# Order of the slabs in the channel stage, and the per-layer gate of the token pair as seven products

## The chip, the cores and the metric

The kernel runs on one core of a Trainium2 chip. The metric is the device time of one execution in microseconds (us); the time given is the median of several runs. The engines are TensorE (PE, matmuls; its weight loads are shown apart as PEld), VectorE (DVE), ScalarE (ACT), GpSimd (POOL) and SyncE (SP), whose queue issues most transfers. They run side by side and wait for each other by semaphores.

## The reference

One layer of a decoder: a mixing part (attention and pooling heads), then a gated feed-forward part, then a per-layer input that is gated by the residual. The change touches the last two.

```python
def _rms(x, g):
    xf = x.astype(jnp.float32)
    y = xf * lax.rsqrt(jnp.mean(xf * xf, axis=-1, keepdims=True) + EPS)
    return (y * g.astype(jnp.float32)).astype(x.dtype)
...
    x = x + _rms(mix, n_mix_post)
    f = _rms(x, n_ffn_pre)
    f = (jax.nn.silu(f @ w_gate) * (f @ w_up)) @ w_down
    x = x + _rms(f, n_ffn_post)
    x = x + jax.nn.sigmoid(x @ w_ple_gate) * (p @ w_ple)
```

The width is 1024, the feed-forward width 2816 (22 chunks of 128), p has 256 columns. 1024 prompt tokens and 32 sample tokens make 1056.

## The kernel before

The tokens stand in the free dimension, as three groups of 352; groups 0 and 1 are called the pair. Activations are kept as halves of 512 features (a tile of 128x1408 is four blocks of 352). Every product is float32 made of three matmuls in a reduced float32 type: an operand is split into a rounded part (ScalarE cast, line 171) and a remainder (VectorE subtraction, line 172), and `gemm` issues hi x hi, hi x lo and lo x hi. So a product over 1024 features of one 128-wide chunk and one group is 24 matmuls of 352 columns. In the names, `wr` is a raw weight, `wh`/`wl` its two parts, `fh`/`fl` those of an activation, `hid` the hidden activations, `pl` those of p, `b` a PSUM bank (there are eight), `o` the sum of the down products, `sg` the gate.

For the pair, gate and up of one chunk are computed together by a scheme with seven half-width products where eight would be needed (84 matmuls in place of 96): the weights' sums S1 to S4 are formed by `w_sums` (line 1001: four 128x512 sums on GpSimd, written over the raw weights, then cast and remainder `sh`/`sl`), the activations' sums T1 to T4 once by `t_sum` (line 960, VectorE). Group 2 uses the plain 24-matmul products. Twenty-two chunks are walked as eleven slabs of two. `WALK` lists which groups take which slab when: with AHEAD = 5, slabs 0 to 4 for group 2 alone, slabs 5 to 10 for all three groups, then slabs 0 to 4 for the pair alone. After a slab, `downs` adds its down products (48 matmuls for each group) to `o`; after the last one of a group it forms squares for the norm, and `ple_steps` makes the residual x2 (a multiply at line 1126, four steps at line 1130 per half), splits it into an operand, and loads and splits p.

Per chunk m and group, `ple_out` then computes the gate (24 matmuls), the embedding product of p (6 matmuls), the sigmoid, a multiply and an add to x2 (lines 1175 to 1181), and writes the output.

Weights come through a list of items in the order of use. `need` keeps four items ahead: it loads a raw weight into one of three `wr` buffers, splits it into two of the eight `wp` tiles, and, for an item of kind "sums", calls `w_sums`. TensorE's instructions stand in the order of the code. The side work (norms, residuals) is written as chains of steps that are handed out between matmuls (`turn`, `chain`), by the VectorE time that `share` grants; VectorE, ScalarE and SyncE execute their queues in the order that the scheduler gave.

Of the kernel before, what the change touches and what calls it, by code (L numbers as in the profile page):

```python
# [10 lines left out]
F32 = mybir.dt.float32  # L11
# [28 lines left out]
AHEAD = 5  # L40
# [21 lines left out]
def trunk_kernel(  # L62
# [158 lines left out]
    WALK += [(s, (0, 1, 2)) for s in range(AHEAD, NSLAB)]  # L221
    WALK += [(s, (0, 1)) for s in range(AHEAD)]
# [6 lines left out]
    def direct_item(src, shape):  # L229
        return item("direct", add_plan(src, shape))  # L230

    WGU, WD = [], []
    for s, gs in WALK:
        pairs_of = []
        for i in range(SLAB):
# [4 lines left out]
            if i == 0 and WD:  # L240
                last_s = WALK[len(WD) - 1][0]
                WD[-1] = [direct_item(w_dn[last_s, j], [P, SLAB, 512]) for j in range(2)]
            if 0 in gs:
                ju = direct_item(w_gu[c, 1], [P, KC, P])
# [4 lines left out]
    WPE = [[], []]  # L249

    def plan_ple(n, m):
        wp = direct_item(w_ple[m // 4], [P, 2, 512]) if m % 4 == 0 else WPE[n][-1][0]
        WPE[n].append((wp, direct_item(w_pg[m], [P, KC, P])))

    FIRST = 1
    for m in range(FIRST):
        plan_ple(0, m)
    WD[-1] = [direct_item(w_dn[WALK[-1][0], j], [P, SLAB, 512]) for j in range(2)]
    for m in range(FIRST, KC):
        plan_ple(0, m)  # L260

    WPE[1] = [None] * 6 + WPE[0][6:]
    wp = WPE[0][-1][0]
    for m in reversed(range(6)):
        if m == 3:
            wp = direct_item(w_ple[0], [P, 2, 512])
        WPE[1][m] = wp, direct_item(w_pg[m], [P, KC, P])

    made = {}

    def need(k, ahead=LOOK):

        for i in range(len(made), min(k + ahead + 1, len(ITEMS))):
            kind, js = ITEMS[i]
            if kind == "direct":
                w_split(js[0])
                made[i] = pairs[js[0]]
            else:
                made[i] = w_sums(*(raws[ITEMS[j][1][0]] for j in js))
            for kind, js in ITEMS[i + 1 : i + 3]:  # L280
                if kind == "direct":
# [626 lines left out]
    def ffn_steps(g):  # L908
# [11 lines left out]
        for h in range(2):  # L920
# [7 lines left out]
            if (g, h) == (1, 0):  # L928
                t_sum("T1")
# [8 lines left out]
        if g == 1:  # L938
            for name in ("T3", "T2", "T4"):
                t_sum(name)  # L940
                yield 20, 0

# [9 lines left out]
    def t_sum(name):  # L952
        (b11, b21), (b12, b22) = ys[0], ys[1]
        out, a, b = {
            "T1": (b11, b12, b11),
            "T3": (b12, b22, b12),
            "T2": (b22, b22, b11),
            "T4": (b21, b21, b22),
        }[name]
        ve.tensor_tensor(out, a, b, op=ALU.subtract)  # L960
        f7[name] = f_operand(out, 0)
# [55 lines left out]
    def gate_up(items, slot, gs, pending):  # L1017
# [270 lines left out]
```

## Time and profile before

| | |
|---|---|
| median of 3 runs | 1115.65 us (1115.2 to 1115.71) |
| profiled execution, span | 1115.2 us |
| granted TensorE clock, by stretches from 350 us on | 1.00 |
| VectorE busy, us per 100, from 400, 600, 800, 900 | 49.0, 54.8, 83.3, 76.8 |
| weight loads of the channel part and the gate (512 KB each) | 64 + 32 + 14 |
| last stretch of the profile with GpSimd work | up to 1000 us |

The trace gives for each engine when an instruction ran and what it waited for. The chain of waits is followed back from the last instruction: at each step to what released it. Groups of instructions have one row for each line, operation and shape, with their number, busy time and mean duration in ns. The matmuls of a TensorE row overlap, so the pace is read from the count in a stretch and not from the mean. GpSimd's first weight sum starts at 386.14 us, with the first slab of all groups; the pair's slabs alone end, and the gate begins, shortly before 1000 us.

### The profile page before, as it was taken

What the parts mean: (1) busy time and instruction counts of PE and PEld (TensorE: products, weight loads), DVE (VectorE), ACT (ScalarE), POOL (GpSimd) and SP (SyncE); (2) the same over time, 40 slices, a digit from 0 to 9 for tenths busy, and PEclk for the clock granted to TensorE, in tenths of its full rate; (3) what the DMA queues carried; (4) which work ended last, traced back from release to release, by engine and by line L of the source; (5) the groups of instructions that cost most, each with busy time, mean ns of one, the idle gap of its engine ahead of it and who ended that gap; (6) DMA issues with size and microseconds to landing.
All of it is one profiled execution on the core that took longest, in us unless ns stands there. A gap on an engine that the chain in (4) does not pass through costs nothing.

```text
span 1115.2 us, 17663 instructions
## 1 busy us (share of the span) xinstructions
PE 1105.2 (99%) x7147; PEld 1089.1 (98%) x7147; DVE 748.6 (67%) x1241; ACT 440.4 (39%) x779; POOL 179.9 (16%) x156
## 2 busy tenths in 40 slices
PE   8999999999999999999999999999999999999998
PEld 8999988899999999999999999999999999999998
DVE  5767478886979955255464555547887877789532
ACT  6423276665645523331221313123424334366220
POOL 0045032200000131011111101111232123100000
PEclk9999999999999999999999999999999999999999
DMA  8121311542543212121110212122112222346211
GB/s 289 58 70 41 121 42 38 195 161 81 209 160 129 98 38 76 39 76 38 39 59 18 78 37 77 38 95 84 57 58 79 73 76 77 118 155 210 85 58 39
DMA packets 35217, 99.54 MB, mean 89 GB/s; under 512 B 4132, under 2 KB 14660, under 8 KB 35136
## 3 DMA queue, kind: packets, MB, share of 16 engines
q1 hardware_dynamic: 33808, 96.65, 25.7%
q10 hardware_dynamic: 1328, 1.77, 0.5%
q8 instruction: 56, 0.92, 0.4%
q14 instruction: 25, 0.20, 0.1%
HBM read 88.30 MB, written 10.11 MB: 88 GB/s over the span
## 4 chain that ended last, share of the span: by engine, by line
PE 94%; DVE 3%; DMA 1%; POOL 1%; issue 0%; ACT 0%; SPq 0%; DVEq 0%; POOLq 0%
PE b L126 93%; PE b L120 1%; DMA a<-in_dmask_dram 1%; DMA xr<-in_x_dram 1%; DVE wl L172 1%; POOL wr L1001 0%; DVE o L1126 0%; DVE x L1130 0%; DVE mx L639 0%; DVE a L747 0%; DVE p L1035 0%; DVE hid L172 0%; POOL a L653 0%; DVE sl L172 0%; ACT sh L171 0%
## 5 line engine op out<-in xcount | busy, mean ns | idle before, releaser
L126 PE MATMUL b<-fh,wh 128*128 128x352 f32 x808 | 260.8, 323 | 0.0
L126 PE MATMUL b<-fl,wh 128*128 128x352 f32 x808 | 258.8, 320 | 0.0
L126 PE MATMUL b<-fh,wl 128*128 128x352 f32 x808 | 258.8, 320 | 0.0
L126 PE MATMUL b<-hid,wh 128*128 128x352 f32 x1056 | 252.6, 322 | 1.8 <-DVE o L1126 1.2
L171 ACT CAST wh<-wr 128x1024 fp32r<-128x1024 f32 (+1 forms) x139 | 142.7, 1030 | 245.3 <-PE b L126 197.1
L172 DVE TENSOR_TENSOR wl<-wr,wh 128x1024 fp32r<-128x1024 f32 (+1 forms) x139 | 170.4, 1229 | 56.2 <-ACT wh L171 52.2
L126 PEld LDWEIGHTS b<-hid,wh 128*128 128x128 f32 x1056 | 182.3, 188 | 2.6 <-issue 1.5
L126 PE MATMUL b<-hid,wl 128*128 128x352 f32 x528 | 169.0, 320 | 0.0
L1001 POOL TENSOR_TENSOR wr<-wr 128x512 f32<-128x512 f32 x44 | 63.3, 1439 | 622.7 <-DVE wl L172 620.9
L126 PEld LDWEIGHTS b<-fl,wh 128*128 128x128 f32 x808 | 151.9, 188 | 0.0
L126 PEld LDWEIGHTS b<-fh,wh 128*128 128x128 f32 x808 | 151.5, 188 | 0.0
L126 PEld LDWEIGHTS b<-fh,wl 128*128 128x128 f32 x808 | 151.4, 187 | 0.0
L1098 DVE TENSOR_TENSOR o<-o,b 128x352 f32<-128x352 f32 x240 | 115.0, 517 | 28.9 <-PE b L126 28.7
L126 PE MATMUL b<-fh,sh 128*128 128x352 f32 x352 | 113.6, 323 | 0.0
L126 PE MATMUL b<-fl,sh 128*128 128x352 f32 x352 | 112.7, 320 | 0.0
L126 PE MATMUL b<-fh,sl 128*128 128x352 f32 x352 | 112.7, 320 | 0.0
L126 PE MATMUL b<-h,wh 128*128 128x352 f32 x480 | 106.0, 326 | 1.7 <-ACT h L372 1.4
L172 DVE TENSOR_TENSOR sl<-wr,sh 128x1024 fp32r<-128x1024 f32 x44 | 53.8, 1223 | 75.9 <-ACT sh L171 75.9
L126 PEld LDWEIGHTS b<-hid,wl 128*128 128x128 f32 x528 | 98.9, 187 | 0.0
L171 ACT CAST sh<-wr 128x1024 fp32r<-128x1024 f32 x44 | 45.7, 1047 | 131.2 <-POOL wr L1001 92.0
L126 PEld LDWEIGHTS b<-h,wh 128*128 128x128 f32 x480 | 82.3, 190 | 3.0 <-ACT h L372 1.8
L126 PE MATMUL b<-h,wl 128*128 128x352 f32 x240 | 66.4, 326 | 0.0
(153 smaller groups left out, 1590.7 us busy)
## 6 DMA issues: line engine op xcount, KB each, us to landing
wr<-in_w_gu_dram SPq DMA_DIRECT2D x64, 512.0 KB, 3.3
wr<-in_w_dn_dram SPq DMA_DIRECT2D x32, 512.0 KB, 3.5
wr<-in_w_pg_dram SPq DMA_DIRECT2D x14, 512.0 KB, 3.5
x<-in_x_dram SPq DMA_DIRECT2D x6, 704.0 KB, 7.0
x1d<-x SPq DMA_DIRECT2D x6, 704.0 KB, 3.5
x<-x1d SPq DMA_DIRECT2D x6, 704.0 KB, 6.6
out_y_dram<-yo SPq DMA_DIRECT2D x24, 176.0 KB, 1.9
wr<-in_w_out_b_dram SPq DMA_DIRECT2D x8, 512.0 KB, 3.3
```

Of the source, the lines that this page charges most:

```text
L120: ins = te.transpose(out, src, ident)
L126: ins = te.matmul(*args, **kw)
L171: fix(se.copy(hi, src))
L172: fix(ve.tensor_tensor(lo, src, hi.bitcast(F32), op=ALU.subtract))
L1001: ge.tensor_tensor(out, a, b, op=op)
L1098: ve.tensor_tensor(o, o, v, op=ALU.add)
```

## The change

AHEAD is 6, and no slab is shared any more: six slabs for group 2 alone, all eleven for the pair alone, then the last five for group 2. `gate_up` is parted into `seven` (the seven products, with a callback for each finished quarter), `gate_up_pair` and `gate_up_one`. For the pair, the second raw weight is split only by half (an item of kind "half", 128x512), since only its last quarter enters a product by itself. The sums T1 to T4 go to GpSimd. The per-layer gate of the pair now uses `seven` too, on two chunks of the gate's weight at a time: `pair_steps` makes x2 of the pair during group 2's last slabs, stores it to memory (`x2d`), forms a second set of T sums (`x27`) and splits their operands; `ple_pair` reads x2 back and runs the embedding product of each quarter (`embed`, 6 matmuls) as it is finished. `ple_pair(0)` comes before group 2's last downs, the other three after them, then `ple_one` does group 2's eight chunks. `share` is 0.35 and 0.5 where it was 0.1 and 0.7.

```diff
-AHEAD = 5
+AHEAD = 6
...
-    WALK += [(s, (0, 1, 2)) for s in range(AHEAD, NSLAB)]
-    WALK += [(s, (0, 1)) for s in range(AHEAD)]
+    WALK += [(s, (0, 1)) for s in range(NSLAB)]
+    WALK += [(s, (2,)) for s in range(AHEAD, NSLAB)]
+    LAST = {g: max(n for n, (_, gs) in enumerate(WALK) if g in gs) for g in range(G)}
...
+    def half_item(src):
+        return item("half", add_plan(src, [P, KC, P]))
...
-                ju = direct_item(w_gu[c, 1], [P, KC, P])
+                ju = half_item(w_gu[c, 1])
...
+    WP2, WPE = [], [None] * KC
+    for i in range(KC // 2):
+        wp = direct_item(w_ple[i // 2], [P, 2, 512]) if i % 2 == 0 else WP2[-1][0]
+        jg = direct_item(w_pg[2 * i], [P, KC, P])
+        ju = half_item(w_pg[2 * i + 1])
+        WP2.append((wp, jg, ju, item("sums", jg, ju)))
+        if i == 0:
+            WD[-1] = dn_items(len(WALK) - 1)
+    LATE = (*range(4, KC), *range(4))
+    for m in LATE:
+        if m == 0:
             wp = direct_item(w_ple[0], [P, 2, 512])
-        WPE[1][m] = wp, direct_item(w_pg[m], [P, KC, P])
+        WPE[m] = wp, direct_item(w_pg[m], [P, KC, P])
...
+            elif kind == "half":
+                w_load(js[0])
+                hl = w_tile([P, 4, P], "wh"), w_tile([P, 4, P], "wl")
+                split(*hl, raws[js[0]][:, 4:8, :])
+                made[i] = hl
...
-                t_sum("T1")
+                t_sum("T1", f7, ys[0], ys[1], flat(ys))
...
-        ve.tensor_tensor(out, a, b, op=ALU.subtract)
-        f7[name] = f_operand(out, 0)
+        ge.tensor_tensor(out, a, b, op=ALU.subtract)
+        b7[name] = f_operand(out, 0)
...
+    def product(w, x):
+        ps = bank()
+        gemm(ps[:, :N], ops4(w, x))
+        turn(12)
+        return ps[:, :N]
+
+    def direct(w, xs2):
+        ps = bank()
+        gemm(ps[:, :N], ops8(w, xs2))
+        turn(24)
+        return ps[:, :N]
+
+    def add(out, a, ps):
+        ve.tensor_tensor(out, a, ps, op=ALU.add)
+
+    def seven(items, x7, done):
 
         ig, iu, is_ = items
-        n = N
-
-        def product(w, x):
-            ps = bank()
-            gemm(ps[:, :n], ops4(w, x))
-            turn(12)
-            return ps[:, :n]
-
-        def direct(w):
-            ps = bank()
-            gemm(ps[:, :n], ops8(w, fs[2]))
-            turn(24)
-            return ps[:, :n]
-
-        def add(out, a, ps):
-            ve.tensor_tensor(out, a, ps, op=ALU.add)
-
         wg = need(ig)
-        if 0 in gs:
-            p1 = tmp(n, "p1")
-            se.copy(p1, product(quarter(wg, 0), f7["B11"]))
-        if 2 in gs:
-            sl = tmp(n, "sl")
-            se.activation(sl, direct(wg), AF.Silu)
-        if 0 in gs:
-            c11 = tmp(n, "c11")
-            add(c11, p1, product(quarter(wg, 1), f7["B21"]))
-            se.activation(c11, c11, AF.Silu)
-        if pending and 0 in gs:
-            pending()
-        wu = need(iu)
-        if 2 in gs:
-            ve.tensor_tensor(sl, sl, direct(wu), op=ALU.mult)
-        for g in gs:
-            if slot == 0:
-                new_hid[g] = half(g, F32R, "hid")
-        if 2 in gs:
-            hid_put(2, slot, sl)
-        if pending and 0 not in gs:
-            pending()
-        if 0 not in gs:
-            return
-        if 2 not in gs:
-            p4 = product(quarter(wu, 1), f7["T4"])
+        p1 = tmp(N, "p1")
+        se.copy(p1, product(quarter(wg, 0), x7["B11"]))
+        c11 = tmp(N, "c11")
+        add(c11, p1, product(quarter(wg, 1), x7["B21"]))
+        done("C11", c11)
+        p4 = product(need(iu), x7["T4"])
         s = need(is_)
-        add(p1, p1, product(s["S2"], f7["T2"]))
-        u3 = tmp(n, "u3")
-        add(u3, p1, product(s["S3"], f7["T3"]))
-        c21 = tmp(n, "c21")
-        if 2 in gs:
-            p4 = product(quarter(wu, 1), f7["T4"])
+        add(p1, p1, product(s["S2"], x7["T2"]))
+        u3 = tmp(N, "u3")
+        add(u3, p1, product(s["S3"], x7["T3"]))
+        c21 = tmp(N, "c21")
         add(c21, u3, p4)
-        ve.tensor_tensor(c21, c21, c11, op=ALU.mult)
-        hid_put(0, slot, c21)
-        p5 = product(s["S1"], f7["T1"])
+        done("C21", c21)
+        p5 = product(s["S1"], x7["T1"])
         add(u3, u3, p5)
         add(p1, p1, p5)
-        add(p1, p1, product(s["S4"], f7["B22"]))
-        se.activation(p1, p1, AF.Silu)
-        ve.tensor_tensor(u3, u3, p1, op=ALU.mult)
-        hid_put(1, slot, u3)
+        done("C22", u3)
+        add(p1, p1, product(s["S4"], x7["B22"]))
+        done("C12", p1)
...
+        def done(which, c):
+            t[which] = c
+            if which in ("C11", "C12"):
+                se.activation(c, c, AF.Silu)
+            if which == "C11":
+                if pending:
+                    pending()
+                for g in (0, 1):
+                    if slot == 0:
+                        new_hid[g] = half(g, F32R, "hid")
+            for g, a, b in ((0, "C21", "C11"), (1, "C22", "C12")):
+                if which == ("C21", "C12")[g]:
+                    ve.tensor_tensor(t[a], t[a], t[b], op=ALU.mult)
+                    hid_put(g, slot, t[a])
+
+        seven(items, f7, done)
...
+    def x2_steps(g, operand):
+
+        for h in range(2):
+            x2[g][h] = half(g, s="x2")
+            nc.sync.dma_start(x2[g][h], x1d[g][h])
+        r = yield from rstd_steps(acc3[g])
+        for h in range(2):
+            yh, xh = os_[g][h], x2[g][h]
+            ve.tensor_tensor(yh, yh, bc4(r), op=ALU.mult)
+            for c in range(4):
+                k = 4 * h + c
+                ve.scalar_tensor_tensor(
+                    xh[:, c, :], yh[:, c, :], gn[:, 3, k : k + 1], xh[:, c, :], op0=ALU.mult, op1=ALU.add
+                )
+                if c % 2:
+                    yield 12, 0
+            operand(g, h, xh)
+            yield 10, 0
...
+    def pair_operand(g, h, xh):
+        nc.sync.dma_start(x2d[g][h], xh)
+        if (g, h) != (1, 0):
+            x27[f"B{h + 1}{g + 1}"] = f_operand(xh, g)
+
+    def pair_steps():
+        for g in (0, 1):
+            yield from x2_steps(g, pair_operand)
+        for name in ("T1", "T2", "T4", "T3"):
+            t_sum(name, x27, x2[0], x2[1], flat(os_))
+            yield 20, 0
+        for g in (0, 1):
+            pl_load(g)
+            yield 6, 0
+
+    def one_steps():
+        x2s[2] = []
+        yield from x2_steps(2, lambda g, h, xh: x2s[2].append(f_operand(xh, g)))
+        pl_load(2)
...
+        if n == LAST[0]:
+            share[0] = 0.35
+            chain(pair_steps(), 19)
+        if n == LAST[2]:
+            chain(one_steps(), 19)
...
-    def ple_out(n, m, g):
+    share[0] = 0.5
+
+
+    def embed(wp, xm, m, g, sg):
+
+        wh, wl = need(wp)
         ph, pl = pls[g]
-        w = WPE[n][m]
-        wh, wl = need(w[0])
         cols = slice((m % 4) * P, (m % 4 + 1) * P)
-        pp, pg = bank(), bank()
-        gemm(pg[:, :N], ops8(need(w[1]), x2s[g]))
-        turn(24)
-        sg = tmp(N, "sg")
...
+    def ple_pair(i):
+
+        wp, *items = WP2[i]
+        if i % 2 == 0:
+            for g in (0, 1):
+                xm[g] = half(g, s="xm")
+                nc.sync.dma_start(xm[g], x2d[g][i // 2])
+
+        def done(which, c):
+            r, g = (int(a) - 1 for a in which[1:])
+            m = 2 * i + r
+            se.activation(c, c, AF.Sigmoid)
+            embed(wp, xm[g][:, m % 4, :], m, g, c)
+
+        seven(items, x27, done)
+
+    def ple_one(m):
+        wp, w = WPE[m]
+        sg = tmp(N, "sg")
+        se.activation(sg, direct(need(w), x2s[2]), AF.Sigmoid)
+        embed(wp, x2[2][m // 4][:, m % 4, :], m, 2, sg)
...
-    hid[:] = new_hid
-    for m in range(FIRST):
-        ple_out(0, m, 2)
-    for m in range(KC):
-        last_down(END, m, 0)
-    chain(ple_steps(0), 24)
-    for m in range(KC):
-        last_down(END, m, 1)
-    chain(ple_steps(1), 54)
-    for m in range(FIRST, KC):
-        ple_out(0, m, 2)
-    finish(chains[:1])
-    for m in reversed(range(KC)):
-        for g in (0, 1):
-            if g == 1 and m == KC - 1:
-                finish(list(chains))
-            ple_out(1, m, g)
...
+    old_hid = list(new_hid)
+    for i in range(KC // 2):
+        ple_pair(i)
+        if i == 0:
+            downs(len(WALK) - 1)
+    finish(list(chains))
+    for m in LATE:
+        ple_one(m)
```

On VectorE, the start of the gate stage, first before: the last pair slab's chunk ends (`u3`, `hid`), three weights are split (`wl`), and the first gate product of group 2 (`sg`, `yo`) stands among the last downs of the pair.

```order
L172 TENSOR_TENSOR wl1505_9642<-wr1490_9535,wh1504_9641 128x1024
L1035 TENSOR_TENSOR p11500_9610<-p11500_9610,b1516_9715 128x352
L172 TENSOR_TENSOR wl1509_9661<-wr1499_9608,wh1508_9660 128x1024
L1079 TENSOR_TENSOR u31512_9680<-u31512_9680,p11500_9610 128x352
L172 TENSOR_TENSOR hid1486_9517<-u31512_9680,hid1486_9517 128x352
L172 TENSOR_TENSOR wl1518_9734<-wr1506_9645,wh1517_9733 128x1024
L1098 TENSOR_TENSOR o765_4716<-o765_4716,b1527_9783 128x352
L1179 TENSOR_TENSOR sg1525_9771<-sg1525_9771,b1520_9739 128x352
L1098 TENSOR_TENSOR o765_4716<-o765_4716,b1529_9793 128x352
L1181 TENSOR_TENSOR yo1526_9780<-sg1525_9771,x21216_7861 128x352
```

Now, at the start of `ple_pair(0)`: `wl1644` is the half split of the pair's second raw weight, `fl` the operands T4 and T3, `sl1646` and `hid1627` the last chunk of group 2, `sl1651` and `sl1653` the remainders of the weight sums, `c11` the first finished quarter, `pl1662` the split of p for group 0.

```order
L172 TENSOR_TENSOR wl1644_10006<-wr1630_9930,wh1643_10005 128x512
L172 TENSOR_TENSOR fl1659_10092<-o790_4762,fh1658_10091 128x1408
L1094 TENSOR_TENSOR sl1646_10011<-sl1646_10011,b1655_10057 128x352
L172 TENSOR_TENSOR fl1661_10097<-o795_4795,fh1660_10096 128x1408
L172 TENSOR_TENSOR hid1627_9923<-sl1646_10011,hid1627_9923 128x352
L172 TENSOR_TENSOR sl1651_10048<-wr1625_9893,sh1650_10047 128x1024
L1041 TENSOR_TENSOR c111676_10141<-p11674_10126,b1677_10142 128x352
L172 TENSOR_TENSOR pl1662_10100<-a1663_10101,pl1662_10100 128x704
L172 TENSOR_TENSOR sl1653_10052<-wr1630_9930,sh1652_10051 128x1024
L1212 TENSOR_TENSOR c111676_10141<-c111676_10141,b1678_10157 128x352
```

The gate stage now has weight sums in it: their remainder `sl1651` stands ahead of the first quarter's add and of the split of p, which stood many rows ahead of the gate before.

On VectorE, the end of group 2's downs at the second gate pair: `acc1699` is the sum of squares of group 2, `sl1715` the remainder of the second pair's weight sums, `c11` that pair's first quarter, and the reciprocal the first step after the norm's 128x1 matmuls.

```order
L1117 TENSOR_TENSOR o540_3287<-o540_3287,b1712_10363 128x352
L803 TENSOR_TENSOR acc1699_10295<-acc1699_10295,sq1709_10349 128x352
L803 TENSOR_TENSOR acc1699_10295<-acc1699_10295,sq1711_10360 128x352
L172 TENSOR_TENSOR sl1715_10379<-wr1670_10118,sh1714_10378 128x1024
L803 TENSOR_TENSOR acc1699_10295<-acc1699_10295,sq1713_10371 128x352
L1041 TENSOR_TENSOR c111726_10413<-p11724_10398,b1727_10414 128x352
L172 TENSOR_TENSOR sl1717_10383<-wr1673_10124,sh1716_10382 128x1024
L319 RECIPROCAL sd1731_10435<-sd1731_10435 128x3
```

The last addition to `acc1699` stands behind `sl1715`; before, no weight sums stood among the last downs.

More of the change, by code (lines that the diff above doesn't have):

```diff
@@ L230, in direct_item, with dn_items @@
         return item("direct", add_plan(src, shape))
+    def half_item(src):
+        return item("half", add_plan(src, [P, KC, P]))
+    def dn_items(n):
+        return [direct_item(w_dn[WALK[n][0], j], [P, SLAB, 512]) for j in range(2)]
     WGU, WD = [], []
@@ L280, in need @@
             for kind, js in ITEMS[i + 1 : i + 3]:
-                if kind == "direct":
+                if kind != "sums":
                     w_load(js[0])
@@ L1082, in trunk_kernel, with gate_up_one @@
+    def gate_up_one(items, slot, pending):
+        ig, iu, _ = items
+        wg = need(ig)
+        sl = tmp(N, "sl")
+        se.activation(sl, direct(wg, fs[2]), AF.Silu)
+        wu = need(iu)
+        ve.tensor_tensor(sl, sl, direct(wu, fs[2]), op=ALU.mult)
+        if slot == 0:
+            new_hid[2] = half(2, F32R, "hid")
+        hid_put(2, slot, sl)
+        if pending:
+            pending()
     os_ = [None] * G
@@ L1102, in trunk_kernel @@
     x2s = [None] * G
+    x27 = {}
     pls = [None] * G
     acc3 = [None] * G
+    x2d = [[dpool.tile([P, 4, NS[g]], F32, name=nm("x2d")) for _ in range(2)] for g in range(2)]
     def last_down(n, m, g):
```

79 lines of the change are left out of this document (21 added, 58 removed).

## The prediction

> **What bounds the kernel now.** First the page's busy line, then the busy time by stretch (`us, PE busy (x) PEld DVE ACT POOL, PEclk, DMA share, GB/s`):
>
> ```profile
> PE 1105.2 (99%) x7147; PEld 1089.1 (98%) x7147; DVE 748.6 (67%) x1241; ACT 440.4 (39%) x779; POOL 179.9 (16%) x156
> ...
> 400.00:500.00 100.00, 100.00 (x631) 100.00 (x630) 48.97 (x79) 33.84 (x56) 15.97 (x12) 1.00 0.17 54
> ...
> 800.00:900.00 100.00, 98.22 (x616) 97.49 (x615) 83.27 (x124) 37.76 (x52) 23.91 (x18) 1.00 0.24 79
> 900.00:1000.00 100.00, 99.56 (x627) 99.04 (x626) 76.78 (x132) 43.03 (x61) 20.55 (x15) 1.00 0.30 103
> 1000.00:1115.00 115.00, 110.98 (x699) 110.68 (x699) 63.09 (x96) 33.66 (x47) 0.00 (x0) 1.00 0.29 100
> ```
>
> TensorE sets the time: in the channel stage it issues 631 matmuls in 100 us without a gap, 0.1585 us each, at the full granted clock. A matmul less is worth 0.1585 us, and a stall of TensorE costs its full length. The stretches 800 to 1000 lack 1.78 + 0.44 = 2.2 us of TensorE. DMA is at 0.17 to 0.30, so the 38 further 512 KB weight loads that the new walk needs (88, 44 and 16 issues of w_gu, w_dn and w_pg, after 64, 32 and 14) cost nothing by themselves. VectorE, at 77 to 83 in the pair stretches, has the least room.
>
> The chain of waits shows how the one long gap arose (start, us, what held the chain), and VectorE's timeline the same place:
>
> ```profile
> 852.06 0.97 issue
> 853.55 1.15 DVE wl L172
> 854.82 1.46 POOL wr L1001
> 856.34 1.48 POOL wr L1001
> 857.89 1.29 POOL wr L1001
> 859.25 1.29 POOL wr L1001
> 860.57 1.06 ACT sh L171
> 861.65 1.23 DVE sl L172
> 862.88 1.54 DVE o L1126
> 864.55 131.55 PE b L126 x828
> ...
> 857.01 0.94 DVE L1098 TENSOR_TENSOR o<-o,b 128x352 f32<-128x352 f32 x2
> 861.65 1.23 DVE L172 TENSOR_TENSOR sl<-wr,sh 128x1024 fp32r<-128x1024 f32 x1 [3.70 <-ACT sh L171]
> ...
> 864.52 0.30 PEld L126 LDWEIGHTS b<-hid,wh 128*128 128x128 f32 x2 [1.47 <-issue]
> ```
>
> When a pair's second raw weight has been split, GpSimd forms the four sums in place, ScalarE rounds, VectorE takes the remainder `sl`: from 854.82 to 862.88, **8.06 us**. VectorE runs its queue in order, so all that stands behind `sl` waits (3.70 us idle); here the o-adds did, banks stayed full, and TensorE lost 1.47 us. That chain is the price I use below.
>
> **The change part by part.** *Matmuls.* The counts of the two kinds of gate and up products before:
>
> ```profile
> L126 PE MATMUL b<-fh,wh 128*128 128x352 f32 x808 | 260.8, 323 | 0.0
> L126 PE MATMUL b<-fh,sh 128*128 128x352 f32 x352 | 113.6, 323 | 0.0
> L126 PE MATMUL b<-pl,wl 128*128 128x352 f32 x48 | 15.4, 320 | 0.0
> ```
>
> The channel products stay the same in number, whichever way the slabs are walked. In the per-layer gate, four pairs of chunks for groups 0 and 1 took 4 x 96 matmuls and take 4 x 84: 48 less (16 of each of the three hi/lo kinds: 808 to 728 with `wh`, 352 to 416 with `sh`), so **-7.6 us**. The embed products stay.
>
> *VectorE, ScalarE, GpSimd.* The prices, with count, busy us and mean ns:
>
> ```profile
> L171 ACT CAST wh<-wr 128x512 fp32r<-128x512 f32 x6 | 3.5, 609 | 1.1 <-DMA wr<-in_w_in_dram 1.1
> L172 DVE TENSOR_TENSOR wl<-wr,wh 128x512 fp32r<-128x512 f32 x6 | 4.0, 686 | 4.4 <-ACT wh L171 4.4
> L172 DVE TENSOR_TENSOR wl<-wr,wh 128x1024 fp32r<-128x1024 f32 x133 | 166.5, 1254 | 51.7 <-ACT wh L171 47.8 <-PE b L126 3.6
> L172 DVE TENSOR_TENSOR fl<-x,fh 128x1408 fp32r<-128x1408 f32 x6 | 9.7, 1622 | 1.1 <-ACT fh L171 1.1
> L172 DVE TENSOR_TENSOR pl<-a,pl 128x704 fp32r<-128x704 f32 x3 | 2.7, 888 | 0.3 <-ACT pl L171 0.3
> L960 DVE TENSOR_TENSOR y<-y,y 128x1408 f32<-128x1408 f32 x4 | 6.5, 1618 | 0.0
> L796 DVE TENSOR_TENSOR acc<-acc,sq 128x352 f32<-128x352 f32 x42 | 22.0, 528 | 8.8 <-ACT sq L795 8.8
> L653 POOL TENSOR_TENSOR a<-a,sm 128x1056 f32<-128x1056 f32 x2 | 3.9, 1946 | 6.7 <-DVE es L643 6.3 <-DVE sm L651 0.4
> ```
>
> VectorE loses four operand sums (6.5 us) and gains 12 full and 26 half weight splits, 8 sum splits and 3 operand splits: 15.0 + 17.8 + 9.8 + 4.9 - 6.5 = 41 us more, out of 1115.2 - 748.6 = 367 free. Spread over the pair slabs this is covered: the half split is 0.57 us shorter than the full one, and the pair stretch 865 to 990 of before, which has the same seven products, ran without a gap. There is no row for a 128x1408 sum on GpSimd: 1.95 us is the lower end, from 1056 columns, twice that the upper; I take 2.6, in proportion to columns. The four sums of f7 fall while group 2 runs alone; those of x27 stand in GpSimd's queue ahead of the gate's first weight sums and fall in group 2's last five slabs, 5 x 144 matmuls or 114 us of TensorE in which GpSimd has nothing else: 8 to 16 us of them are covered. The Trainium skill ("GPSIMD Engine Reference", section 3.1, side-by-side accounting) measures a GpSimd add at 1.96 times VectorE's, which would make these sums 3.2 us each, an estimate; that cover would hold them too.
>
> *The gate stage.* Its first part is 480 matmuls, 76.1 us: four times 84 + 24, and group 2's last downs. In it VectorE has 126 instructions, 81 us by the mean durations of before; as two o-adds took 0.94 us together, successive ones overlap by some 0.09 and it is nearer 70. So VectorE has no room left there, and each weight sum chain makes it idle besides. I count from t = 0, the first product of the first gate pair, and follow the four chains. None starts early: w_ple holds two of the eight tiles of split weights, and the half split of a pair's second weight must wait for a tile that TensorE still reads.
>
> (A) The tile comes free 24 matmuls before t = 0, at -3.8. With 0.61 and 0.69 of half cast and split, the sums start at -2.5 at best, -1.5 in VectorE's order, and the first `sl` ends at 5.6 to 6.6. Behind it stand the C11 add and the split of `pl` (0.45 + 0.85), and the first embed product needs `pl` at 24 x 0.1585 = 3.8: a stall of 3.1 to 4.1 us. Two operand splits lie beside these sums, and such a neighbourhood costs:
>
> ```profile
> 386.14 4.58 POOL L1001 TENSOR_TENSOR wr<-wr 128x512 f32<-128x512 f32 x1 [169.35 <-DVE wl L172]
> 393.53 1.28 POOL L1001 TENSOR_TENSOR wr<-wr 128x512 f32<-128x512 f32 x1
> 386.41 3.16 DVE L172 TENSOR_TENSOR fl<-y,fh 128x1408 fp32r<-128x1408 f32 x2
> ```
>
> A sum next to two operand splits took 4.58 us where it takes 1.28 alone: 3.3 more. So 3.1 to 7.4; I take **4.5**, as ScalarE hands the two splits over apart. The Trainium skill ("SBUF — State Buffer", section "Who interferes with whom") has this as an exclusive lock: a VectorE instruction with two SBUF inputs and a GpSimd instruction that reads SBUF wait for each other, the earlier first. In the row the sum began before the splits and yet came last, so who wins isn't settled by that; by the rule in full both splits delay the chain and A is 7.3.
>
> (B) The next half split waits for the fourth down of group 2 (t = 25.1, and B's own clock moves with A): 25.1 + 0.61 + 0.69 + 8.06 = 34.5 for its `sl`. Behind it on VectorE stands the last square sum of group 2 (0.53), and TensorE needs that for the reciprocal norm right after the pair's second product, at 32.7: 2.2 us; with the late read of x2 (704 KB, 6.6 us to landing in the row below) ahead of it on VectorE up to 5. I take **3.3**.
>
> ```profile
> x<-x1d SPq DMA_DIRECT2D x6, 704.0 KB, 6.6
> L1130 DVE SCALAR_TENSOR_TENSOR x<-o,c,x 128x352 f32<-128x352 f32 x24 | 15.0, 664 | 0.0
> ```
>
> (C) The third pair's tile comes free with the last product of the second pair: 0.61 + 0.69 + 8.06 = 9.4 later `sl` is there, and TensorE has 48 matmuls until it needs it, 7.6: **1.8** (1.7 to 2.5).
>
> (D) The fourth pair's half split stands behind group 2's residual chain (a 128x1408 multiply, four steps of 0.66, an operand split: 1.6 + 2.7 + 1.6): between 0 and 5.9, I take **2.5**.
>
> Sum 12.1, between 7.0 and 20.8. Where group 2 starts its last five slabs, the pair's last downs put 30 adds and square sums and 3 splits on VectorE, 30 x 0.47 + 3 x 1.16 = 17.6 us in 96 matmuls, 15.2 us; the eight banks take some of that: 0 to 2.4, **1.0**. The gaps of before, 2.2, hang on the old order (residual chains among the downs) and go: **-2.2** (-1.5 to -3). The eight direct gates of group 2 at the end have one weight split for 30 matmuls, and the tail is the same.
>
> Total: -7.6 + 12.1 + 1.0 - 2.2 = +3.3, from 1115.2 of the profiled execution 1118.5. The median of the runs is 0.45 above that execution, so I forecast **1119 us**; with all low ends 1112, with all high ends 1130.
>
> **The rivals.** *Covered.* If the chains start earlier than the tiles' order tells, or VectorE's later work is not in the way, the stalls shrink to nothing: -7.6 - 2.2 + 1 gives 1106.9; with half of the low ends 1110. For it: the 131.55 us without a gap in the chain quoted above, in which such chains were covered. Against: there every second chunk brings a slab's 96 down matmuls, 15.2 us, over which a chain runs; here 9.4 us have 7.6. Faster.
>
> *No gain in the end.* Stalls at their low ends (7.0) with the old gaps gone: -7.6 + 7.0 + 1 - 2.2, near 1114: half of this case is within the noise.
>
> *VectorE as the bound of the gate stage.* Here the mechanism is not a single late tile but the queue: 81 us of work without overlap and four times the 3.70 us idle at an `sl` make 96 us for 76.1 of TensorE. Then the loss is 20: -7.6 + 20 + 1 - 2.2 = +11.2, or 1127 in the median. It decides once VectorE's busy and blocked time in the stage is over 76.1 + 7.6 + 2.2 = 86; with overlap it is 70 + 15 = 85. For it speaks the 83.27 that VectorE already had in 800 to 900 beside the gap there; against, that overlap. Slower.
>
> **How the numbers follow.** Forecast, with its own range 1112 to 1126: 0.55. Covered: 0.20. No gain in the end: 0.10. VectorE as the bound: 0.15. What a measurement of this kernel can tell is about 0.2%, 2.2 us: 1113.4 to 1117.9 is no change. Of the forecast 0.05 lies below that, 0.10 in it, 0.40 above; of covered all is faster; of no gain 0.04 faster and 0.06 the same; the last all slower. Faster 0.29, same 0.16, slower 0.55. The range 1109 to 1126 leaves out the fully covered case and the upper end of the VectorE case.
>
> **What would show it.** The count of `fh,wh` at 728 and `fh,sh` at 416. TensorE gaps in the gate stage: one before the first embed product (A), one before the 128x1 matmuls of the norm in the second pair (B), one ahead of the S2 products of the third and fourth (C, D), each released by `sl`, `pl` or `acc` on VectorE with GpSimd's four sums before it; VectorE over 85% busy there. I am wrong if the gate stage shows under 7 us of gaps, or if gaps of more than 1 us stand in the pair slabs, which I cost at nothing.

## The result and the profile after

The changed kernel takes **1130.65 us** in the median (1128.0 to 1137.11, four runs) against 1115.68 of the kernel before (four runs): a ratio of 1.0141, 95% interval 1.0111 to 1.0171. It is slower, as forecast, but by 15 us instead of 3, and outside the range of 1109 to 1126.

The page's line of busy times of the kernel after, and its busy time by stretch (us, busy time and count of PE, PEld, DVE, ACT and POOL, granted TensorE clock, DMA share, GB/s):

```profile
PE 1105.7 (98%) x7099; PEld 1088.3 (96%) x7099; DVE 828.6 (73%) x1314; ACT 480.8 (43%) x832; POOL 233.1 (21%) x180
```

```profile
300.00:400.00 100.00, 98.40 (x620) 98.12 (x619) 88.52 (x113) 53.09 (x65) 14.62 (x4) 1.00 0.44 147
800.00:900.00 100.00, 100.00 (x633) 100.00 (x632) 74.92 (x123) 43.50 (x66) 16.17 (x12) 1.00 0.33 110
900.00:1000.00 100.00, 92.15 (x578) 91.48 (x577) 85.03 (x106) 43.25 (x51) 23.98 (x8) 0.97 0.47 162
1000.00:1130.00 130.00, 117.94 (x703) 116.21 (x703) 86.44 (x135) 46.72 (x68) 17.83 (x12) 0.96 0.42 139
```

There are 48 matmuls less, and TensorE is busy 0.5 us longer than before. The stretch 800 to 900, which lacked 1.78 us, is full. Apart from 1.6 us between 300 and 400, what is lost lies behind 900: TensorE stands idle, and the granted clock, 1.00 in the stretches shown of before, is 0.97 and 0.96. TensorE's waits (us in total, times, longest):

```profile
PE b L126 <- ACT pl L171: 7.8, 1, 7.8
PE b L126 <- DVE acc L803: 3.3, 1, 3.3
PE b L126 <- ACT sh L171: 2.3, 2, 1.5
PE b L126 <- DVE o L1117: 1.6, 1, 1.6
...
PE b L126 <- DVE sl L172: 1.3, 2, 0.7
...
PE b L126 <- DVE pl L172: 0.8, 1, 0.8
```

These are the four places of the forecast (`pl`: A; `acc`: B; `sh` and `sl`: C and D) and one that was costed at nothing (`o`, at 354, where the pair slabs begin). From the differences between successive matmul starts, less the 0.1585 us of one matmul, the 14.9 us between the two profiled executions (1130.1 and 1115.2) come out so:

| item | us |
|---|---|
| 48 matmuls less | -7.6 |
| gaps of before, gone (at 816, 863, 999) | -3.0 |
| new gap at 354 | +1.8 |
| A, from 991.2 (7.93 + 1.31 + 0.30) | +9.5 |
| B, at 1026.8 | +3.4 |
| C, at 1052.9 (1.69 + 0.84) | +2.5 |
| D, at 1073.1 (0.98 + 0.84) | +1.8 |
| matmuls at half clock behind A, B and D (1.3 + 1.6 + 1.8) | +4.7 |
| sum; not placed | 13.1; 1.8 |

**Gap A.** VectorE's timeline ahead of it (start, us, operation, output and inputs, idle time before and what ended it):

```profile
968.30 3.56 DVE L172 TENSOR_TENSOR hid<-sl,hid 128x352 fp32r<-128x352 f32 x1
971.78 4.25 DVE L172 TENSOR_TENSOR wl<-wr,wh 128x1024 fp32r<-128x1024 f32 x1
...
985.21 3.15 DVE L172 TENSOR_TENSOR fl<-o,fh 128x1408 fp32r<-128x1408 f32 x2
988.28 0.68 DVE L172 TENSOR_TENSOR wl<-wr,wh 128x512 fp32r<-128x512 f32 x1
988.89 1.61 DVE L172 TENSOR_TENSOR fl<-o,fh 128x1408 fp32r<-128x1408 f32 x1
...
990.85 2.28 DVE L172 TENSOR_TENSOR fl<-o,fh 128x1408 fp32r<-128x1408 f32 x1
...
998.20 1.23 DVE L172 TENSOR_TENSOR sl<-wr,sh 128x1024 fp32r<-128x1024 f32 x1 [3.57 <-ACT sh L171]
...
999.78 0.89 DVE L172 TENSOR_TENSOR pl<-a,pl 128x704 fp32r<-128x704 f32 x1
```

GpSimd's timeline over the same time, three of the sums for the operands T and then the four weight sums:

```profile
963.32 3.97 POOL L971 TENSOR_TENSOR o<-x,o 128x1408 f32<-128x1408 f32 x1 [7.72 <-DVE x L1144]
967.25 4.23 POOL L971 TENSOR_TENSOR o<-x,x 128x1408 f32<-128x1408 f32 x1
971.44 3.51 POOL L971 TENSOR_TENSOR o<-x,o 128x1408 f32<-128x1408 f32 x1
...
989.04 2.61 POOL L1012 TENSOR_TENSOR wr<-wr 128x512 f32<-128x512 f32 x1 [14.09 <-DVE wl L172]
991.73 4.02 POOL L1012 TENSOR_TENSOR wr<-wr,wr 128x512 f32<-128x512 f32 x2
995.83 1.26 POOL L1012 TENSOR_TENSOR wr<-wr 128x512 f32<-128x512 f32 x1
```

And ScalarE's, first the half cast that goes ahead of the half split:

```profile
983.78 0.62 ACT L171 CAST wh<-wr 128x512 fp32r<-128x512 f32 x1 [1.08 <-PE b L126]
...
997.12 1.04 ACT L171 CAST sh<-wr 128x1024 fp32r<-128x1024 f32 x1 [5.67 <-POOL wr L1012]
...
998.42 0.78 ACT L171 CAST pl<-a 128x704 fp32r<-128x704 f32 x1
```

While GpSimd runs the T sums, VectorE's `hid` takes 3.56 us for a tile of 352 columns, and a full split 4.25 where 1.25 is its mean in the forecast's rows: both engines have work and neither gets on. The half cast ends at 984.40, but VectorE comes to the half split at 988.28 only, behind two operand splits (985.21, 3.15 us); its end releases the weight sums. Two more operand splits then run beside the sums: from 989.04 to ScalarE's `sh` at 997.12 they take 8.1 us, where the same four took 5.75 in the forecast's chain (854.82 to 860.57). TensorE waits from 991.3 on for p's upper half, which stands behind `sh` on ScalarE, and then for its lower half, which stands behind `sl` on VectorE.

**Gap B.** The last addition to group 2's square sum (`acc`) stands behind the second pair's `sl`, as in the forecast's order; VectorE's timeline:

```profile
1028.67 1.23 DVE L172 TENSOR_TENSOR sl<-wr,sh 128x1024 fp32r<-128x1024 f32 x1 [2.25 <-ACT sh L171]
1029.81 0.52 DVE L803 TENSOR_TENSOR acc<-acc,sq 128x352 f32<-128x352 f32 x1
```

**The clock.** Five stretches of the kernel after (columns as above): two behind A, one behind B, one over C and one over D:

```profile
1000.00:1004.00 4.00, 3.28 (x11) 3.29 (x12) 3.12 (x4) 2.59 (x4) 0.00 (x0) 0.50 0.71 223
1004.00:1008.00 4.00, 4.00 (x27) 4.00 (x26) 1.82 (x3) 1.05 (x1) 0.00 (x0) 1.00 0.97 397
1031.00:1035.00 4.00, 4.00 (x17) 4.00 (x18) 3.38 (x8) 2.66 (x4) 0.00 (x0) 0.57 0.76 254
...
1052.00:1057.00 5.00, 2.81 (x16) 2.23 (x16) 2.23 (x2) 3.31 (x5) 1.58 (x2) 1.00 0.05 11
1072.00:1079.00 7.00, 5.50 (x23) 4.92 (x22) 4.76 (x7) 3.67 (x5) 1.10 (x1) 0.76 0.37 106
```

Behind A the clock is at one half: matmuls start 0.293 us apart until 1003.8, then 0.1585 again. The same follows B and D; C passes without it. Each such stretch adds 1.3 to 1.8 us to a gap.

### The profile page after: what moved, and what is told of

It is laid out like the page before. It is cut to its first block, busy times and chain, and to the rows that moved or that the text cites. A ratio compares the mean times of both kernels' runs of the same rounds, so it can differ in the third digit from the quotient of the medians.

```text
span 1130.1 us, 17901 instructions
## 1 busy us (share of the span) xinstructions
PE 1105.7 (98%) x7099; PEld 1088.3 (96%) x7099; DVE 828.6 (73%) x1314; ACT 480.8 (43%) x832; POOL 233.1 (21%) x180
## 5 line engine op out<-in xcount | busy, mean ns | idle before, releaser
L171 ACT CAST wh<-wr 128x1024 fp32r<-128x1024 f32 (+1 forms) x177 | 171.7, 971 | 254.9 <-PE b L126 182.1
L172 DVE TENSOR_TENSOR wl<-wr,wh 128x1024 fp32r<-128x1024 f32 (+1 forms) x177 | 214.5, 1218 | 65.2 <-ACT wh L171 59.5
L126 PE MATMUL b<-fh,wh 128*128 128x352 f32 x728 | 236.1, 324 | 1.6 <-DVE o L1117 1.6
L126 PE MATMUL b<-fh,wl 128*128 128x352 f32 x728 | 234.0, 321 | 0.0
L126 PE MATMUL b<-fl,wh 128*128 128x352 f32 x728 | 234.0, 321 | 0.0
L126 PE MATMUL b<-fh,sh 128*128 128x352 f32 x416 | 135.1, 325 | 2.3 <-ACT sh L171 2.3
L126 PEld LDWEIGHTS b<-fh,wl 128*128 128x128 f32 x728 | 137.0, 188 | 0.0
L126 PE MATMUL b<-fh,sl 128*128 128x352 f32 x416 | 134.1, 322 | 1.3 <-DVE sl L172 1.3
L126 PE MATMUL b<-fl,sh 128*128 128x352 f32 x416 | 133.9, 322 | 0.0
L126 PEld LDWEIGHTS b<-fh,sh 128*128 128x128 f32 x416 | 78.5, 189 | 2.9 <-ACT sh L171 2.9
```

Of the source, the lines that this page charges most:

```text
L126: ins = te.matmul(*args, **kw)
L171: fix(se.copy(hi, src))
L172: fix(ve.tensor_tensor(lo, src, hi.bitcast(F32), op=ALU.subtract))
```

## The experiments

Times in brackets are of the kernel before, run on the same chip beside it. "Gate gaps" are TensorE's gaps from 940 us on, read as in the table.

**1. Two more tiles for split weights.** The forecast laid gap A on a late tile.

```diff
-        return wpool.tile(shape, F32R, tag="wp", bufs=2 * W_PAIRS, name=nm(s))
+        return wpool.tile(shape, F32R, tag="wp", bufs=2 * W_PAIRS + 2, name=nm(s))
```

> The changed kernel with ten tiles for split weights in place of eight, nothing else. Tile theory (the weight sums of a gate pair start late because the half split waits for a tile that TensorE still reads): the first gate pair's half split comes ahead of the three operand splits, the gap before the first embed product falls from 9.5 us to 0 to 3, the gaps ahead of the S2 products of the third and fourth pairs (2.5 and 2.0) go, the half-clock stretches behind the gaps go with them; 1114 to 1120 us. Rival, VectorE as the bound of the gate stage: its work is the same, so the gaps only move; the stage still loses over 15 us and the time stays above 1124.

Measured: 1129.34 us in two runs (1116.67), ratio 1.0117, 1.0097 to 1.0137: no gain that these intervals can tell. Gap A is 11.6 us. VectorE's timeline of this run:

```profile
981.42 0.68 DVE L172 TENSOR_TENSOR wl<-wr,wh 128x512 fp32r<-128x512 f32 x1
982.02 6.87 DVE L172 TENSOR_TENSOR fl<-o,fh 128x1408 fp32r<-128x1408 f32 x3
```

its GpSimd timeline:

```profile
982.18 2.60 POOL L1012 TENSOR_TENSOR wr<-wr 128x512 f32<-128x512 f32 x1 [9.88 <-DVE wl L172]
984.86 5.15 POOL L1012 TENSOR_TENSOR wr<-wr,wr 128x512 f32<-128x512 f32 x2
990.09 1.26 POOL L1012 TENSOR_TENSOR wr<-wr 128x512 f32<-128x512 f32 x1
```

and ScalarE's:

```profile
998.38 0.78 ACT L171 CAST pl<-a 128x704 fp32r<-128x704 f32 x1 [2.06 <-DMA a<-in_p_dram]
```

The half split comes 6.9 us earlier (4.2 us against the gate's first product, which itself begins 2.7 us earlier here), so the tile did hold it. But the sums now meet three operand splits and take 9.2 us, and p arrives late: its load was issued at 994.09 only, behind two loads of w_dn that held SyncE's queue for 19.07 us. The gaps at C and D gave way to one of 3.1 us at 1062. An earlier tile alone moves the collision and gains nothing; what it would be worth with p on time isn't shown by this run.

**2. p ahead of the operands.** The load and split of p for each group go right behind its steps for x2, ahead of the T sums.

```diff
         for g in (0, 1):
             yield from x2_steps(g, pair_operand)
+            pl_load(g)
+            yield 6, 0
         for name in ("T1", "T2", "T4", "T3"):
             t_sum(name, x27, x2[0], x2[1], flat(os_))
             yield 20, 0
-        for g in (0, 1):
-            pl_load(g)
-            yield 6, 0
```

> The changed kernel with p loaded and split for the pair right after each group's residual, ahead of the T sums. Theory that the weight sum chain sets the first gap and the split of p is only what stands behind it: the gap moves from the first embed product to the S2 product 18 matmuls later and falls from 9.5 us to 6 to 7 (the sum's remainder ends at the same time, TensorE does 2.9 us more before it needs it); 1125 to 1129 us. Rival, the late load and split of p is the cause: the gap goes, 1118 to 1121 us.

Measured: 1127.36 us in one run (1116.67). The wait for `pl` is gone, and the next user of the chain has it: the first product with `sh` stands 5.82 us, and 7.1 with the short gaps behind it.

```profile
PE b L126 <- ACT sh L171: 8.2, 3, 5.7
```

So p's place in the queues makes some 2.5 us of A; in the rest TensorE waits for the weight sums, which take 8.1 us here too (987.90 to 995.99).

**3. The gate's weight sums on VectorE.**

```diff
-                made[i] = w_sums(*(raws[ITEMS[j][1][0]] for j in js))
+                made[i] = w_sums(*(raws[ITEMS[j][1][0]] for j in js), ve if i >= WP2[0][1] else ge)
...
-            ge.tensor_tensor(out, a, b, op=op)
+            eng.tensor_tensor(out, a, b, op=op)
```

> The changed kernel with the gate stage's weight sums (16 of 128x512) on VectorE instead of GpSimd; the channel stage's stay. Chain theory (the length of the chain from half split to remainder, some 8 us and up to 10.4 beside operand splits, sets the gaps): four sums take 2.4 to 2.7 us on VectorE, no exclusion between the two engines, the chain becomes 5 to 8 us, the gaps fall from 17.5 to about 9 us in all; 1118 to 1123 us. Rival, VectorE as the bound: 10 us more of work on it lengthens the stage, 1133 to 1142 us.

Measured: 1120.83 us in one run (1116.67). Gate gaps are 9.5 us instead of 17.3: A 7.4, and none over 0.8 at B, C and D. VectorE got 16 instructions more and the kernel became 10 us faster: VectorE's work is not the bound of the gate stage, and the chain through GpSimd is the larger part of the loss; A keeps 7.4 us without it.

**4. The walk alone.** The pair's gate in the plain form of 24 matmuls per product, as before, without weight sums and T operands in it; the slabs in the new order. It has 48 matmuls more than the change.

```diff
-    for i in range(KC // 2):
-        wp = direct_item(w_ple[i // 2], [P, 2, 512]) if i % 2 == 0 else WP2[-1][0]
-        jg = direct_item(w_pg[2 * i], [P, KC, P])
-        ju = half_item(w_pg[2 * i + 1])
-        WP2.append((wp, jg, ju, item("sums", jg, ju)))
+    for m in range(KC):
+        wp = direct_item(w_ple[m // 4], [P, 2, 512]) if m % 4 == 0 else WP2[-1][0]
+        WP2.append((wp, direct_item(w_pg[m], [P, KC, P])))
...
-    def ple_pair(i):
+    def ple_two(m):
...
+        for g in (0, 1):
+            sg = tmp(N, "sg")
+            se.activation(sg, direct(need(w), x2s[g]), AF.Sigmoid)
+            embed(wp, xm[g][:, m % 4, :], m, g, sg)
```

> The changed kernel with the plain per-layer gate for the pair (24 matmuls for each chunk and group, no T sums and no weight sums in the gate; x2 still stored and read again, p still split late): 48 matmuls or 7.6 us more than the changed kernel. Theory that the whole loss lies in the gate's weight sum chains and the new walk is worth some 1 us: no gap over 1 us in the gate stage except perhaps one before the first embed product, 1113 to 1117 us. Rival, the walk itself costs (more weight splits, T sums on GpSimd, the late residual chain): 1119 us or more.

Measured: 1115.4 us in ten runs (1116.67), ratio 0.9997, 0.9981 to 1.0012. The gate has 0.3 us of gaps. The wait of 1.6 us for `o` where the pair's slabs begin remains, as the channel stage's own T sums are still on GpSimd here. So the walk, with those sums, is worth nothing that can be told, and the loss lies in the seven-product gate: it saves 7.6 us and costs some 22.

**5. Operands handed out earlier.** The `share` of VectorE's time by which the chains of steps are handed out, 0.6 instead of 0.35, moves the T operands away from the gate's first sums.

```diff
-            share[0] = 0.35
+            share[0] = 0.6
```

> The changed kernel with share at 0.6 in place of 0.35 while group 2's last slabs run: the pair's residual, T sums, operand splits and split of p are handed out earlier; nothing else. Theory that the first gap came from what stood around the first weight sum chain (two operand splits ahead of the half split, two more beside GpSimd's sums, the split of p behind): the chain is 8.1 us by itself, its remainder ends before the S2 products, the first gap (9.5 us) goes to 0 to 1 and the half clock behind it goes; the other gaps (3.4, 2.5, 1.8) stay: 1117 to 1121 us. Rival, the late tile: the first gap stays at 3 us or more, 1122 to 1126 us.

Measured: 1127.91 us in one run (1116.05), a miss. A is gone, and a new gap of 6.9 us stands at 947.5, in group 2's slabs. VectorE's timeline there:

```profile
945.35 4.21 DVE L172 TENSOR_TENSOR fl<-o,fh 128x1408 fp32r<-128x1408 f32 x1
949.49 4.16 DVE L172 TENSOR_TENSOR wl<-wr,wh 128x1024 fp32r<-128x1024 f32 x1
953.57 0.51 DVE L172 TENSOR_TENSOR hid<-sl,hid 128x352 fp32r<-128x352 f32 x1
```

and GpSimd's:

```profile
943.46 4.62 POOL L971 TENSOR_TENSOR o<-x,x 128x1408 f32<-128x1408 f32 x1
948.03 4.54 POOL L971 TENSOR_TENSOR o<-x,o 128x1408 f32<-128x1408 f32 x1
```

TensorE's wait names `hid`, which itself takes 0.51 us; it came late because the two splits ahead of it took 4.21 and 4.16 us beside T sums. The forecast had this at nothing: the T sums are not covered in either place where they were tried.

**6. Both engines' roles, in combinations.** Experiments 3 and 5 together:

> As the run before, and the gate's weight sums on VectorE. If both parts of the theory hold (operands early removes the first gap, the shorter chain the other three), the gate stage has under 2 us of gaps and the 48 matmuls show: 1115.7 - 7.6 - 3.0 (gaps of before that are gone) + 1.8 (new gap where the pair's slabs begin) = 1107, with 1106 to 1111 allowed. Rival, VectorE as the bound of the gate stage (10 us more on it): gaps of 5 us and more remain, 1114 us or above.

Measured: 1118.91 us in nine runs (1116.05), ratio 1.0025, 1.0015 to 1.0035: a miss, and its 6.9 us at 947, with 1.4 us at half clock behind them, say most of why, since the T sums were still on GpSimd; the gate stage itself has 1.8 us of gaps. With two more tiles as well:

> As the run before, and ten tiles for split weights. If late tiles hold nothing once the chain is short and the operands early, the same time as the run before within 1 us. If they do, the gaps left ahead of the S2 products go, 1 to 2 us less. A third possibility, as with ten tiles alone: earlier splits put the weight loads of the downs ahead of others in SyncE's queue and a new gap of some 3 us comes.

Measured: 1121.78 us in six runs (1116.05), ratio 1.0055, 1.0034 to 1.0077: the tiles make it no better here either; four gaps of 0.5 to 1.6 us came at 1042 to 1062. Then the T sums too on VectorE:

```diff
-        ge.tensor_tensor(out, a, b, op=ALU.subtract)
+        ve.tensor_tensor(out, a, b, op=ALU.subtract)
```

First alone, then with the share of 0.6, then with the share and the weight sums on VectorE:

> The changed kernel with the operand sums T back on VectorE, nothing else. Theory: VectorE gets 7.5 us back that it waited on GpSimd between 965 and 976 us and spends some 5 there on the sums, so the first gate pair's half split comes 2 to 3 us earlier and the first gap falls from 9.5 to 6 to 8; the gap where the pair's slabs begin (1.8) goes; the other gate gaps stay: 1124 to 1128 us. Rival, moving them to GpSimd saved VectorE's time: the first gap grows, 1131 us or more.

> The changed kernel with share at 0.6 and the operand sums T on VectorE; the gate's weight sums stay on GpSimd. Theory: no first gap and none in group 2's last slabs; the gaps of the second to fourth gate pair (2.9, 2.5, 1.8, with some 2 to 3 us at half clock) stay, since only they hang on the length of the weight sum chain: 1116 to 1119 us, and the difference to the run with all sums on VectorE is what that chain costs, 7 to 10 us.

> The changed kernel with share at 0.6, the gate's weight sums and all operand sums T on VectorE (the channel stage's weight sums stay on GpSimd). Theory: GpSimd's 128x1408 sums (3.2 to 4.6 us each) hold up VectorE's instructions with two inputs in SBUF, so that they cost VectorE more than the 1.6 us each that they take on it; on VectorE the gap of 6.6 us that the two runs with early operands showed in group 2's last slabs goes with its half clock (1.4), and the 1.8 us where the pair's slabs begin: 1118.9 - 6.9 - 1.4 - 1.8 = 1109, allowed 1107 to 1111, less than the kernel before. Rival, that gap comes from VectorE's load (0.6 hands out too much at once): 6.5 us more of work on VectorE make it as long or longer, 1117 us or above.

Measured: 1128.0, 1116.97 (one run each; 1118.16) and **1109.12 us** in five runs (1118.16), ratio 0.9914, 0.990 to 0.9927. The last beats both kernels. Last, the same with the old share:

> The run with all sums on VectorE, but share at the changed kernel's 0.35: operands and p are handed out late again. Theory: the chain from half split to remainder is some 5 us instead of 8 to 10, but two operand splits still stand ahead of the half split and the split of p behind the remainder, so 2 to 4 us of the first gap come back, and its half clock perhaps: 1111 to 1115 us. Rival, on VectorE the sums alone are enough and the early hand-out was only needed against GpSimd: 1108 to 1110 us.

Measured: 1115.18 us in ten runs (1116.47), ratio 0.999, 0.998 to 0.9999, just above what was expected. The eight combinations, as the difference in us from the kernel before on the same chip, gate gaps behind the stroke. Four cells are of one run each (T alone on VectorE at both shares, the weight sums alone at 0.35, all on GpSimd at 0.6), and runs of one kernel lie 2 to 9 us apart, so differences of 1 to 3 us are not shown to be more than that:

| share | all sums on GpSimd | T on VectorE | weight sums on VectorE | both on VectorE |
|---|---|---|---|---|
| 0.35 | +15.0 / 17.3 | +9.8 / 14.6 | +4.2 / 9.5 | -1.3 / 7.0 |
| 0.6 | +11.9 / 14.2 | -1.2 / 7.0 | +2.9 / 8.7 | **-9.0** / 2.1 |

Handing the operands out earlier is worth 8 to 11 us where the T sums are on VectorE, and 1 to 3 where they are on GpSimd, since there the gap only moves to 947. The weight sums' place is worth 8 to 11 us in all four pairs. The fastest one's page and stretches, to be held against those of after:

```profile
PE 1100.8 (99%) x7099; PEld 1083.6 (98%) x7099; DVE 828.7 (75%) x1338; ACT 481.4 (43%) x832; POOL 176.7 (16%) x156
```

```profile
900.00:1000.00 100.00, 100.00 (x632) 100.00 (x632) 88.08 (x121) 48.47 (x58) 0.00 (x0) 1.00 0.60 209
1000.00:1109.00 109.00, 103.72 (x638) 101.45 (x636) 82.14 (x134) 41.54 (x61) 0.00 (x0) 1.00 0.37 122
```

VectorE has 24 instructions more than in the changed kernel and is busy 0.1 us longer: GpSimd's help had saved it nothing. Its timeline at the first weight sums:

```profile
983.04 0.69 DVE L1012 TENSOR_TENSOR wr<-wr 128x512 f32<-128x512 f32 x1
983.77 1.42 DVE L1012 TENSOR_TENSOR wr<-wr,wr 128x512 f32<-128x512 f32 x2
985.22 0.69 DVE L1012 TENSOR_TENSOR wr<-wr 128x512 f32<-128x512 f32 x1
987.11 1.22 DVE L172 TENSOR_TENSOR sl<-wr,sh 128x1024 fp32r<-128x1024 f32 x1 [0.76 <-ACT sh L171]
```

The chain from the first sum to the end of `sl` takes 5.3 us here, 10.4 in the kernel after (989.04 to 999.43).

## Why the prediction was right in direction and wrong in size

**Matmuls, -7.6:** right; the counts are 728 and 416, as said:

```profile
L126 PE MATMUL b<-fh,wh 128*128 128x352 f32 x728 | 236.1, 324 | 1.6 <-DVE o L1117 1.6
...
L126 PE MATMUL b<-fh,sh 128*128 128x352 f32 x416 | 135.1, 325 | 2.3 <-ACT sh L171 2.3
...
L971 POOL TENSOR_TENSOR y<-y,y 128x1408 f32<-128x1408 f32 x4 | 14.6, 3655 | 153.8 <-issue 133.6 <-DVE y L931 13.6 <-DVE fl L172 6.5
```

**The step that failed** first is the cover of the T sums, "8 to 16 us of them are covered". Their length was the smaller error: the last row above has the first four at 3.66 us, within the bounds of 1.95 to 3.9; the other four (3.51 to 4.53) have a mean of 4.1. TensorE's matmuls were counted as the work that hides these sums, while the sums hold up VectorE's splits, for which those matmuls wait. The forecast had the row that shows it (a sum of 4.58 us beside two operand splits) and used it for the weight sums of A only. The gap at 947 shows it: the three runs with T on GpSimd and the share of 0.6 have it, and the two with T on VectorE and that share have none. In the kernel after, the T sums make the 1.8 us at 354 and, by the run with T alone on VectorE (A 7.0), some 2.6 of the 5.0 us that A is too long. VectorE, forecast to be 41 us busier, was 80.0 us busier (828.6 after 748.6), and 825.0 with the T sums back on it; the rest of that difference is not traced. Two more terms were mis-sized, A itself and the price of a stall:

**A, 4.5 (3.1 to 7.4): 9.5.** In the forecast's clock t = 0 is 24 x 0.1585 before the first embed product was due (991.3), so 987.5. The sums were to start at -1.5; they started at 989.04, 3.0 us late. They took 8.1 us for 5.75 in the forecast's chain, 2.3 more, where the neighbourhood had been given up to 3.3. With the forecast's 4.1 for a start at -1.5 that makes 9.4. The tile is not the reason for the 3.0 us: it came free as forecast, and the half cast began at 983.78, t = -3.7. What failed is "-1.5 in VectorE's order", which allows 1.0 us: two operand splits of 3.15 us stood ahead of the half split, and the list in "The change" begins behind them. "The half split must wait for a tile that TensorE still reads" holds, as experiment 1 showed by moving it, but with the tile free A remains. It goes when the operands are handed out early, with the weight sums still on GpSimd (experiment 5): what stood ahead of the half split and beside the sums made A twice its forecast. The first wait was on ScalarE, where p's upper half stands behind `sh`, and only the 1.3 us behind it on VectorE, where the forecast had looked.

**B 3.3, C 1.8, D 2.5** measured 3.4, 2.5 and 1.8: right in place and in their sum, each behind a weight sum chain. That the sum fits to 0.2 us is in part luck, as C stands at its upper end and D 0.7 below its value; and the longer wait of C and of D ended with ScalarE's `sh`, where the forecast named VectorE. Experiment 3 left none over 0.8 us by taking GpSimd out of the chain.

**Left out: the clock.** The forecast let a stall cost "its full length". It costs more: 4.7 us in sum. The forecast gave 1118.5 for the profiled execution, which took 1130.1. The 11.6 us between are A's excess of 5.0, the clock's 4.7, 1.8 at 354 and the 1.8 not placed, less 1.0 and 0.8 of the two terms below; B, C and D together were 0.2 off.

**Start of group 2's last five slabs, +1.0:** no gap there. "Gaps of more than 1 us in the pair slabs, which I cost at nothing" was named as what would make me wrong: there is one, of 1.76 us, at 354. VectorE's and GpSimd's timelines:

```profile
351.58 3.92 DVE L172 TENSOR_TENSOR wl<-wr,wh 128x1024 fp32r<-128x1024 f32 x1
```

```profile
351.19 3.23 POOL L971 TENSOR_TENSOR y<-y,y 128x1408 f32<-128x1408 f32 x1 [133.60 <-issue]
```

A split beside a T sum again; in the two versions with T alone on VectorE (share 0.35 and 0.6) this gap is gone, while B and C are there as before.

**Gaps of before, -2.2:** measured -3.0, at the upper end given.

**The rivals.** VectorE as the bound of the gate stage came nearest in time (1127) for a wrong reason: experiment 3 and the fastest version give VectorE more to do in the stage and are faster. Nor was VectorE over 85% busy there, as the forecast expected: 76.2 of the 98.5 us from 987.5 to 1086, 77%. The covered case (1107 to 1110) is what the change reaches with its sums on VectorE and its operands early: 1109.12, and 9.0 us under the kernel before on the same chip.

The rule that the forecast weighed, that of the Trainium skill ("SBUF — State Buffer", section "Who interferes with whom"), that a VectorE instruction with two SBUF inputs and a GpSimd instruction that reads SBUF exclude each other, agrees with these rows: 3.56 us for a `hid` that takes 0.51 alone, and 3.5 to 4.6 for the sums beside it. The `hid` ends at 971.86, 0.4 us behind the sum that ran beside it (to 971.48), and the full split at 976.03, 1.1 us behind the next (to 974.95): each did about its own work once the sum was over.

## What to carry to other kernels

Work given to an engine that looks idle is covered only if it doesn't share a resource with an engine whose results are waited for: look in the trace for one place where the two meet, and price all instructions by that row. A chain across engines costs what stands behind its last instruction on each in-order queue that it blocks, ScalarE's as well as VectorE's. A TensorE stall of a few us can cost half as much again in clock, so price a short one above its length.

## What the runs showed of the hardware that was not expected

Half clock followed short gaps. Behind D, 0.98 and 0.84 us of idle 0.4 us apart were enough: 1072 to 1079 has a mean granted clock of 0.76, and some 11 matmuls started 0.293 us apart. C, with 1.69 + 0.84 us, passed at 1.00 in this execution; in the experiment with T alone on VectorE and the share of 0.6, the same gap of 2.5 us was followed by half clock. The gap of 1.76 us at 354 was not. The Trainium skill ("TensorE: Matmul & The Clock Gate", "What's actually happening") puts the fall to half rate behind at least one idle window of about 3.4 us that runs free. That phase decides fits these runs, and the some 3.2 us for which half clock lasted are near that window; that a whole window must be idle does not, since two gaps of 1.8 us together sufficed.

Two engines that met took longer than one doing both jobs. Eight T sums cost GpSimd 30.9 us, and VectorE, relieved of them and of the gate's weight sums, was busy as long as with them.

Open: 1.8 us of the 14.9 are not placed; some stretches, 1056 to 1073 among them, run at 0.161 us a matmul at full granted clock. Which of two colliding instructions goes first, and why the fastest version keeps 2.1 us of short gaps in the gate, was not tried. Each variant also got its queue orders anew from the scheduler, so a swap of engines changes some order too; that part was not held fixed.
